# Three sparsely used experts of a mixture layer: fp32 products in column tiles, and expert matrices stored in 1 MB blocks

## The chip, the cores and the metric

The kernel runs on one core of one Trainium2 chip. The metric is device time in microseconds (us) of one execution of the whole program, the median of several runs. A profile of one execution gives the rows below.

## The reference, cut to what matters

The program is a four-layer network on 256 tokens of width 1024, all in fp32: two hybrid layers, a pooling layer with a dense feed-forward part, and an attention layer with a mixture of eight experts. The change is in the mixture alone:

```python
def moe_ffn(x, router, w_gu, w_down):        # D = 1024, N_EXPERTS = 8, TOP_K = 2, D_FF_EXPERT = 3584
    logits = (xt @ router).astype(jnp.float32)
    top_v, top_i = lax.top_k(logits, TOP_K)
    w = jax.nn.softmax(top_v, axis=-1)
    combine = jnp.einsum('tk,tke->te', w, jax.nn.one_hot(top_i, N_EXPERTS, ...))
    for e in range(N_EXPERTS):
        y = y + combine[:, e:e + 1] * swiglu(xt, w_gu[e], w_down[e])

def swiglu(x, w_gu, w_down):
    g, u = jnp.split(x @ w_gu, 2, axis=-1)
    return (jax.nn.silu(g) * u) @ w_down
```

Each expert has 42 MB of weights (w_gu 1024 x 7168, w_down 3584 x 1024), so all eight are 336 blocks of 1 MB (1,048,576 bytes). The router, evaluated on the inputs, gives the experts 63, 135, 103, 26, 69, 94, 6 and 16 tokens. The kernel takes expert 0 first (63 tokens) and sorts the rest by count: positions 0 to 7 hold 63, 135, 103, 94, 69, 26, 16 and 6 tokens.

## The kernel before

A product of fp32 matrices is made of single-pass products of split numbers. `wload` (L133) loads 1 MB of weights into a tile `raw` [128, 2048]. `wsplit` copies it in a reduced format into `whi` on ScalarE (L148) and subtracts on VectorE to get the rest, `wlo` (L149). `raw` has five buffers, `whi` and `wlo` four each. `mm3` (L182 to L184) then takes three matmuls of 512 columns: activation-hi by whi, activation-hi by wlo, activation-lo by whi. That is how tiles of 128 tokens (kind "f") work. A tile of 64 tokens (kind "h") puts the 64 hi and the 64 lo columns of its activations side by side into one stationary operand, so that two matmuls do (`prod`, L1284 and L1285); `fold` then adds the upper 64 PSUM rows to the lower (a copy on ScalarE, L1292, an add on VectorE, L1293).

An expert goes through seven chunks of 512 hidden columns. A chunk has three parts, each with two 1 MB blocks: `up1` (gate product and silu), `up2` (the other product and the multiplication, after `mid` has transposed the chunk before, L1353) and `down` (into the PSUM banks `acc`, two chunks later). This text calls one such part a step: two blocks, 24 matmuls for a tile of 128 tokens, 16 for one of 64. An expert has 21 steps. `gather` (L1253) picks an expert's tokens by a product with a selection matrix, `weigh` and `combine` (L1396 to L1409) scale its result and add it to `y`.

Experts at positions 0 to 4 have an "f" tile; the one at position 1 has an "h" tile as well (its tokens 129 to 192). Positions 5, 6 and 7 have "h" tiles. `run_experts` is a generator that stops after each step. The driving loop runs positions 0, 7, 1, 2, 3, 4 in this order, and a second generator, `light`, holds positions 5 and 6: it is advanced by two steps behind each step of position 1, and by one behind each of position 2. All blocks are loaded from SyncE's queue, in program order; a load waits there until the buffer that it writes is free. Beside the five `raw` buffers a list `K.spare` gives some loads a buffer elsewhere, during position 0 alone.

A block of w_gu is four pieces of 512 columns, so each partition gets rows of 2 KB; one of w_down is two rows of 4 KB per partition.

If a count is over a table `lim`, a branch runs more tiles. The counts above are under it in both kernels, so the branch is not taken.

Of the kernel before, what the change touches and what calls it, by code (L numbers as in the profile page):

```python
# [51 lines left out]
def _consts():  # L52
# [36 lines left out]
    for g in range(2):  # L89
        for q in range(64):  # L90
# [10 lines left out]
                ("lim", np.array([[128.0, 192, 128, 256, 256, 64, 256, 256]])),  # L101
# [58 lines left out]

class W:
# [10 lines left out]
    def __call__(self, k, c0, c1):  # L172
        hi, lo = self.parts[k // self.per]
        return hi[:, k % self.per, c0:c1], lo[:, k % self.per, c0:c1]

# [962 lines left out]
def route_order(K, pool, S):  # L1138
# [34 lines left out]
    R = wide(pool, 48, 192 + 448, name="R").rearrange("p (a b) -> p a b", a=6)  # L1173
# [16 lines left out]
class Tile:  # L1190


    def __init__(self, s0, kind):
        self.s0, self.kind = s0, kind
        self.xg, self.P, self.sb, self.sg, self.hT = None, None, False, {}, {}
# [11 lines left out]
def select(K, pool, R, p, tl, tiles=(0, 1)):  # L1207
# [5 lines left out]
    m = 64 if tl.kind == "h" else 128  # L1213
# [14 lines left out]
def gather_x(K, pool, x, R, p, tl, n, between=None):  # L1228
# [4 lines left out]
    m = 64 if half else 128  # L1233
    xg = buffer(K, pool, f"xg{n}", 0, [128, KT, m // 64, 128], F32R, dbl)
# [10 lines left out]
    for k, t in steps:  # L1245
# [12 lines left out]
        if half:  # L1258
# [6 lines left out]
def gather_w(K, pool, cw, p, tl, n):  # L1265
# [9 lines left out]
    tl.cs = K.csp.tile([128, 1], F32, name=f"cs{n}", bufs=dbl)  # L1275
# [14 lines left out]
def fold(K, a, ps):  # L1290

    K.nc.scalar.activation(a, ps[64:128, :], AF.Copy)  # L1292
    K.nc.vector.tensor_tensor(a, ps[0:64, :], a, op=OP.add)  # L1293
    return a


class Expert:
    def __init__(self, p, tiles, n0=0):
        self.p, self.tiles, self.n0 = p, [Tile(*t) for t in tiles], n0
        self.static = 0 if p == 0 else None  # L1300


def run_experts(K, pool, A, x, R, ri, cw, y, experts, hook=None, last=False):
# [5 lines left out]
    def begin(E):  # L1309
# [5 lines left out]
        E.gu = A["moe_w_gu_2"][0][ds(e, 1), :, :].rearrange("o (k p) n -> p (o k) n", p=128)  # L1315
        E.dn = A["moe_w_down_2"][0][ds(e, 1), :, :].rearrange("o (k p) n -> p (o k) n", p=128)
        for n, tl in enumerate(E.tiles):
            tl.n = E.n0 + n
# [6 lines left out]
    def up1(E, f):  # L1325
        w = W(K, E.gu[:, :, f * 512:(f + 1) * 512], KT, 512)
        for tl in E.tiles:
            ps = bank(K, "mm")
            for k in range(KT):
                prod(K, tl, ps, tl.xg[:, k], w(k, 0, 512), k == 0, k == KT - 1)  # L1330
            m = 64 if tl.kind == "h" else 128
            a = buffer(K, pool, f"sg{tl.n}", E.p * NF + f, [128, 512], F32, 2)
            nc.scalar.activation(a[:m], fold(K, a[:64], ps) if m == 64 else ps, AF.Silu)
            tl.sg[f] = a

    def up2(E, f):
        w = W(K, E.gu[:, :, FE + f * 512:FE + (f + 1) * 512], KT, 512)
        for tl in E.tiles:
            ps = bank(K, "mm")
            for k in range(KT):  # L1340
                prod(K, tl, ps, tl.xg[:, k], w(k, 0, 512), k == 0, k == KT - 1)
            m = 64 if tl.kind == "h" else 128
# [298 lines left out]
```

## Time and profile before

| | us |
|---|---|
| median of 3 runs | 2108.87 (2108.22 to 2114.42) |
| the profiled execution | 2108.73 |
| its span | 2106.8 |
| first matmul of an expert | 1098.6 |
| last addition to y, start | 2088.8 |
| PE busy | 2039.0 (97%) |
| VectorE (DVE) busy | 1605.5 (76%) |
| ScalarE (ACT) busy | 1255.6 (60%) |

The times of the trace are counted from the start of the span. The busy share of PE is not its use: matmul records overlap in the pipeline, so use has to be read from the distance between their starts.

### The profile page before, as it was taken

The page shows a single profiled execution, that of the slowest core. Times are in us where ns is not written, and L with a number is a line of the kernel's source. Part 1 is how long each engine was busy: PE and PEld are TensorE (multiplying, and loading weights), DVE is VectorE, ACT ScalarE, POOL GpSimd, SP SyncE. Part 2 cuts the span into 40 slices and gives each one's busy share as a digit, 9 for nine tenths or more (in the row PEclk, how much of TensorE's full clock was granted, in tenths as well). Part 3 has the DMA queues.
Part 4 walks back from the last instruction along what each step waited for, and adds up shares of the span by engine and source line. Part 5 has one row for each costly group of instructions (what it writes and reads, how often), then busy time and mean ns, then how long its engine had stood idle before and what let it go on. Part 6 is the DMA issues. An engine that isn't in the chain of part 4 may idle for free. (4 is left out here: it accounts for less than half of the span.)

```text
span 2106.8 us, 28987 instructions
## 1 busy us (share of the span) xinstructions
PE 2039.0 (97%) x11351; PEld 1742.8 (83%) x11351; DVE 1605.5 (76%) x1820; ACT 1255.6 (60%) x1345; POOL 35.2 (2%) x39
## 2 busy tenths in 40 slices
PE   8999999999999999999999999999999999999996
PEld 7879997888998899898788877778777878888885
DVE  7865545876555644566779899999999999898887
ACT  6644444655444444354437787887777876777773
POOL 0000000000001100000000000000000000000000
PEclk9999999999999999999989999999999999999998
DMA  8434554535555455550349979999999999999995
GB/s 312 141 100 150 174 197 165 171 121 180 187 180 192 161 186 194 162 197 21 125 160 326 357 289 374 351 371 354 365 344 326 371 366 337 345 354 351 339 366 182
DMA packets 237954, 523.75 MB, mean 249 GB/s; under 512 B 12016, under 2 KB 44144, under 8 KB 237680
## 3 DMA queue, kind: packets, MB, share of 16 engines
q1 hardware_dynamic: 237664, 521.75, 69.9%
q8 instruction: 91, 1.49, 0.3%
q14 instruction: 55, 0.45, 0.1%
q10 hardware_dynamic: 144, 0.07, 0.0%
HBM read 520.73 MB, written 1.05 MB: 248 GB/s over the span
## 5 line engine op out<-in xcount | busy, mean ns | idle before, releaser
L149 DVE TENSOR_TENSOR wlo<-raw,whi 128x2048 fp32r<-128x2048 f32 (+2 forms) x482 | 1046.1, 2193 | 265.0 <-ACT whi L148 264.6
L148 ACT ACTIVATE whi<-raw 128x2048 fp32r<-128x2048 f32 (+2 forms) x484 | 877.6, 1839 | 328.1 <-issue 70.5
L183 PE MATMUL acc<-wlo,hT 128*128 128x512 f32 x624 | 244.6, 392 | 2.7 <-DVE wlo L149 2.7
L184 PE MATMUL acc<-whi,hT 128*128 128x512 f32 x624 | 242.7, 389 | 0.0
L182 PE MATMUL mm<-xT,whi 128*128 128x256 f32 (+1 forms) x824 | 237.2, 288 | 0.8 <-ACT mqk L424 0.4
L184 PE MATMUL mm<-xT,wlo 128*128 128x256 f32 (+1 forms) x824 | 234.7, 285 | 0.0
L183 PE MATMUL mm<-xT,whi 128*128 128x256 f32 (+1 forms) x824 | 233.8, 284 | 0.3
L182 PE MATMUL acc<-whi,hT 128*128 128x512 f32 x624 | 233.2, 390 | 0.0
L183 PE MATMUL mm<-wlo,xg 128*128 128x512 f32 x448 | 176.5, 394 | 0.8 <-DVE wlo L149 0.8
L182 PE MATMUL mm<-whi,xg 128*128 128x512 f32 x448 | 175.9, 393 | 0.0
L184 PE MATMUL mm<-whi,xg 128*128 128x512 f32 x448 | 174.8, 390 | 0.2 <-DVE xg L198 0.2
L182 PEld LDWEIGHTS mm<-xT,whi 128*128 128x128 f32 (+1 forms) x824 | 155.5, 189 | 4.5 <-issue 1.1
L183 PEld LDWEIGHTS mm<-xT,whi 128*128 128x128 f32 (+1 forms) x824 | 155.6, 189 | 3.7 <-DVE xT L643 1.1
L184 PEld LDWEIGHTS mm<-xT,wlo 128*128 128x128 f32 (+1 forms) x824 | 155.6, 189 | 1.3 <-issue 0.7
L183 PEld LDWEIGHTS acc<-wlo,hT 128*128 128x128 f32 x624 | 117.2, 188 | 28.7 <-DVE wlo L149 5.6
L184 PEld LDWEIGHTS acc<-whi,hT 128*128 128x128 f32 x624 | 117.2, 188 | 24.1
L182 PEld LDWEIGHTS acc<-whi,hT 128*128 128x128 f32 x624 | 117.2, 188 | 24.0
L183 PE MATMUL mx<-xT,whi 128*128 128x256 f32 x416 | 117.7, 283 | 0.0
L184 PE MATMUL mx<-xT,wlo 128*128 128x256 f32 x416 | 117.7, 283 | 0.0
L182 PE MATMUL mx<-xT,whi 128*128 128x256 f32 x416 | 117.7, 283 | 0.0
L1285 PE MATMUL mm<-wlo,box 128*128 128x512 f32 x280 | 107.5, 392 | 0.0
L1284 PE MATMUL mm<-whi,box 128*128 128x512 f32 x280 | 107.3, 390 | 0.0
(397 smaller groups left out, 3417.2 us busy)
## 6 DMA issues: line engine op xcount, KB each, us to landing
raw<-in_moe_w_gu_dram SPq DMA_DIRECT2D x207, 1024.0 KB, 6.8
raw<-in_moe_w_down_dram SPq DMA_DIRECT2D x106, 1024.0 KB, 6.8
raw<-in_w_up_dram SPq DMA_DIRECT2D x32, 1024.0 KB, 5.8
raw<-in_w_down_dram SPq DMA_DIRECT2D x32, 1024.0 KB, 5.1
raw<-in_w_in_dram SPq DMA_DIRECT2D x26, 1024.0 KB, 5.5
raw<-in_ffn_w_gu_dram SPq DMA_DIRECT2D x22, 1024.0 KB, 5.0
spare<-in_moe_w_gu_dram SPq DMA_DIRECT2D x17, 1024.0 KB, 7.2
raw<-in_ffn_w_down_dram SPq DMA_DIRECT2D x11, 1024.0 KB, 4.7
```

Of the source, the lines that this page charges most:

```text
L148: nc.scalar.activation(h, d, AF.Copy)
L149: K.lo.tensor_tensor(l, d, h.bitcast(F32), op=OP.subtract)
L182: nc.tensor.matmul(ps, l[0], r[0], start=start, stop=False)
L183: nc.tensor.matmul(ps, l[0], r[1], start=False, stop=False)
L184: nc.tensor.matmul(ps, l[1], r[0], start=False, stop=stop)
L1284: nc.tensor.matmul(ps, x[:, 0, :], w[0], start=start, stop=False)
L1285: nc.tensor.matmul(ps, x[:, 0, :], w[1], start=False, stop=stop)
```

## The change

The experts at positions 5, 6 and 7 no longer split their weights. Position 5 has a tile of 64 tokens (kind "s"), 6 and 7 have tiles of 32 (kind "q"). Their matmuls take the raw fp32 weights and fp32 activations directly (`prod_full`, L1327), one for each 128 rows by 512 columns of weights: 8 matmuls in a step. The output of successive matmuls goes to different PSUM partitions: two places of 64 rows, or four of 32, which is a place of its own in the columns of the PE array. `fold` adds these parts up. All three now stand in `light`, and a fraction says how many light steps follow a step of each heavy expert: 0.4 for position 0 (once the first light tile is gathered), 1.35 for position 1, 0.45 for 2 to 4. What is left comes behind position 4. The spare list gives every ninth load an extra buffer over the whole layer. The host lays the expert matrices out so that each 1 MB block is contiguous, 8 KB per partition.

```diff
-                ("lim", np.array([[128.0, 192, 128, 256, 256, 64, 256, 256]])),
+                ("lim", np.array([[128.0, 192, 128, 256, 256, 64, 32, 256]])),
...
+class Raw:
+    def __init__(self, K, src, kt, n):
+        self.per = min(kt, 2048 // n)
+        self.parts = [wload(K, src[:, k:k + self.per, :], self.per, n) for k in range(0, kt, self.per)]
...
+        self.m = {"f": 128, "h": 64, "s": 64, "q": 32}[kind]
+        self.full = kind in "sq"
...
+def prod_full(K, tl, ps, c, x, w, start, stop):
+    K.nc.tensor.matmul(ps[tl.m * c:tl.m * c + tl.m], x, w, start=start, stop=stop)
...
+def fold(K, pool, a, ps, m=64):
     K.nc.scalar.activation(a, ps[64:128, :], AF.Copy)
     K.nc.vector.tensor_tensor(a, ps[0:64, :], a, op=OP.add)
-    return a
+    if m == 32:
+        b = pool.tile([32, 512], F32, name="fq")
+        K.nc.scalar.activation(b, a[32:64], AF.Copy)
+        K.nc.vector.tensor_tensor(a[0:32], a[0:32], b, op=OP.add)
+    return a[:m]
...
     def up1(E, f):
-        w = W(K, E.gu[:, :, f * 512:(f + 1) * 512], KT, 512)
+        w = (Raw if E.full else W)(K, E.gu[f], KT, 512)
         for tl in E.tiles:
             ps = bank(K, "mm")
             for k in range(KT):
-                prod(K, tl, ps, tl.xg[:, k], w(k, 0, 512), k == 0, k == KT - 1)
+                if tl.full:
+                    G = 128 // tl.m
+                    prod_full(K, tl, ps, k % G, tl.xg[:, k], w(k, 0, 512), k < G, k >= KT - G)
+                else:
+                    prod(K, tl, ps, tl.xg[:, k], w(k, 0, 512), k == 0, k == KT - 1)
...
     def down(E, f):
-        w = W(K, E.dn[:, f * 4:f * 4 + 4, :], 4, 1024)
+        w = (Raw if E.full else W)(K, E.dn[:, f * 4:f * 4 + 4, :], 4, 1024)
         for tl in E.tiles:
+            if tl.full:
+                if f == 0:
+                    tl.acc = [bank(K, "acc") for _ in range(2)]
+                for k in range(4):
+                    for h in range(2):
+                        if tl.m == 32:
+                            prod_full(K, tl, tl.acc[h], 2 * (k % 2) + (h ^ (k // 2)), tl.hT[f][:, k],
+                                      w(k, h * 512, (h + 1) * 512), f == 0, f == NF - 1)
...
-            for q in range(5):
-                for n in range(q > 0, 5):
+            for q in range(44):
+                for n in range(q > 0, 5 if q < 2 else 2):
...
-            E = [Expert(p, t) for p, t in enumerate(([F0], [F0, H(128)], [F0], [F0], [F0], [H(0)], [H(0)], [H(0)]))]
+            E = [Expert(p, t) for p, t in enumerate(([F0], [F0, H(128)], [F0], [F0], [F0], [(0, "s")], [(0, "q")], [(0, "q")]))]
...
-            light = go([E[5], E[6]])
-            for e, f in go([E[q] for q in (0, 7, 1, 2, 3, 4)], hook, True):
-                for _ in range({1: 2, 2: 1}.get(e.p, 0)):
-                    next(light, None)
+            light, done, due = go([E[5], E[6], E[7]]), 0, 0.0
+            rate = (0.4, 1.35, 0.45, 0.45, 0.45)
+            for q, (e, f) in enumerate(go([E[q] for q in (0, 1, 2, 3, 4)], hook, True)):
+                if E[5].tiles[0].xg is not None:
+                    due += rate[e.p]
+                while done < int(due) and next(light, None):
+                    done += 1
+            for _ in light:
+                pass
...
+    a["moe_gu"] = f(np.asarray(inputs["moe_w_gu_2"])[0].reshape(NE, 2, 4, 128, 14, 512)
+                    .transpose(0, 4, 1, 3, 2, 5).reshape(NE, 14, 2, 128, 2048))
+    a["moe_dn"] = f(np.asarray(inputs["moe_w_down_2"])[0].reshape(NE, 14, 2, 128, 1024)
+                    .transpose(0, 1, 3, 2, 4).reshape(NE, 14, 128, 2048))
```

The instructions of the layers ahead of the mixture keep their order on every engine. Inside it, three places show what moves. The first is PE in the expert of position 1, before: `xgr` are the activations of its "f" tile, `box` those of an "h" tile in `light`, `xg` its own "h" tile.

```order
L1284 MATMUL mm<-whi,xg_11451 128x512
L1285 MATMUL mm<-wlo,xg_11451 128x512
L182 MATMUL mm<-whi,xgr_11032 128x512
L1284 MATMUL mm<-whi,box_10899 128x512
L1353 MATMUL mm<-ident,box_10900 128x64 x4
L183 MATMUL mm<-wlo,xgr_11032 128x512
L184 MATMUL mm<-whi,xgr_11032 128x512
```

The same expert after the change (L1318 and L1319 are now the "h" tile's two matmuls, L210 to L212 the "f" tile's three, L1407 the transposes, L1284 the gathering, L1327 the fp32 products on raw weights):

```order
L1318 MATMUL mm<-whi,box_10276 128x512
L1319 MATMUL mm<-wlo,box_10276 128x512
L1407 MATMUL mm<-ident,box_10277 128x64 x4
L1327 MATMUL mm<-raw,box_10278 64x512 x4
L1327 MATMUL mm<-spare_11037,box_10278 64x512 x4
L1327 MATMUL mm<-raw,box_10278 64x512 x8
L1284 MATMUL mm<-P,x 128x32 x16
L1304 MATMUL mm<-identr,Pr 128x128 x2
L1306 MATMUL mm<-cw,Pr 128x2 x2
L1407 MATMUL mm<-ident,sg_10753 128x128 x4
```

So a light step is 8 matmuls in place of 16 (here two steps stand behind each other); they stand in runs between the heavy tile's matmuls, 106 such runs in all.

The second place is PE at the end of the layer. Before, the last rows ahead of the branch are those of position 4 and its combination:

```order
L182 MATMUL acc<-whi,hT_17109 128x512
L183 MATMUL acc<-wlo,hT_17109 128x512
L184 MATMUL acc<-whi,hT_17109 128x512
L1407 MATMUL mm<-ye,PT_15994 128x512 x2
L1408 MATMUL mm<-ye,PT_15994 128x512 x2
```

After, the light steps that are left stand behind them (L1481 and L1482 are the combination):

```order
L1482 MATMUL mm<-ye,PT_14664 128x512 x2
L1327 MATMUL mm<-raw,box_10278 32x512 x8
L1407 MATMUL mm<-ident,box_10277 128x32 x4
L1327 MATMUL mm<-raw,box_10278 32x512 x8
L1327 MATMUL acc<-raw,hTl 32x512 x4
L1407 MATMUL mm<-ident,box_10277 128x32 x4
L1327 MATMUL acc<-raw,hTl 32x512 x4
L1327 MATMUL acc<-spare_16221,hTl 32x512 x4
L1327 MATMUL acc<-raw,hTl 32x512 x12
L1481 MATMUL mm<-ye,PTl_11093 128x512 x4
L1482 MATMUL mm<-ye,PTl_11093 128x512 x4
```

The third place is SyncE's queue in the middle of the layer, with what each load waits for (register instructions between the loads are left out). Before, the buffer of a load was always last read by VectorE:

```order
L133 DMA raw<-in_moe_w_gu_dram 128x4x512 [waits DMAHW1_49,DVE_49]
L133 DMA raw<-in_moe_w_gu_dram 128x4x512 [waits DMAHW2_49,DVE_49]
L133 DMA raw<-in_moe_w_down_dram 128x2x1024 [waits DMAHW3_49,DVE_49]
L133 DMA raw<-in_moe_w_down_dram 128x2x1024 [waits DMAHW4_49,DVE_49]
L133 DMA raw<-in_moe_w_gu_dram 128x4x512 [waits DMAHW5_49,DVE_49]
```

After, a load into a buffer that held a light block waits for PE:

```order
L133 DMA raw<-in_moe_gu_dram 128x2048 [waits DMAHW7_49,DVE_49]
L133 DMA raw<-in_moe_dn_dram 128x2048 [waits DMAHW0_49,PE_49]
L133 DMA raw<-in_moe_dn_dram 128x2048 [waits DMAHW1_49,PE_49]
L133 DMA raw<-in_moe_gu_dram 128x2048 [waits DMAHW2_49,DVE_49]
L133 DMA raw<-in_moe_gu_dram 128x2048 [waits DMAHW3_49,DVE_49]
L133 DMA raw<-in_moe_dn_dram 128x2048 [waits DMAHW5_49,DVE_49]
L133 DMA raw<-in_moe_dn_dram 128x2048 [waits DMAHW6_49,PE_49]
```

## Rows read from the trace of the kernel before

**Rows 1.** The page: the span in 40 slices (granted PE clock in tenths, GB/s).

```profile
PEclk9999999999999999999989999999999999999998
DMA  8434554535555455550349979999999999999995
GB/s 312 141 100 150 174 197 165 171 121 180 187 180 192 161 186 194 162 197 21 125 160 326 357 289 374 351 371 354 365 344 326 371 366 337 345 354 351 339 366 182
```

**Rows 2.** Busy us (and instructions) of each engine in stretches of the mixture.

```profile
core 0: us, PE busy (x) PEld busy (x) DVE busy (x) ACT busy (x) POOL busy (x), PEclk, DMA share, GB/s
1250.00:2050.00 800.00, 786.73 (x3630) 640.22 (x3629) 734.35 (x519) 600.12 (x460) 0.00 (x0) 1.00 0.98 354
...
1326.00:1650.00 324.00, 319.97 (x1446) 256.34 (x1445) 303.66 (x224) 249.92 (x204) 0.00 (x0) 1.00 0.98 354
...
1760.00:2060.00 300.00, 300.00 (x1391) 248.33 (x1391) 260.25 (x158) 213.47 (x146) 0.00 (x0) 1.00 0.97 352
```

**Rows 3.** Who waited for whom, 1760 to 2060 us (total, times, longest).

```profile
DVE wlo L149 <- ACT whi L148: 29.9, 39, 3.0
ACT whi L148 <- PE mm L184: 22.5, 28, 2.6
...
ACT whi L148 <- DMA raw<-in_moe_w_gu_dram: 2.3, 3, 1.4
```

**Rows 4.** Groups by line, 1760 to 2060 us: busy, mean ns, idle before.

```profile
L149 DVE TENSOR_TENSOR wlo<-raw,whi 128x2048 fp32r<-128x2048 f32 x101 | 228.4, 2287 | 30.1 <-ACT whi L148 29.9
L148 ACT ACTIVATE whi<-raw 128x2048 fp32r<-128x2048 f32 x101 | 191.5, 1915 | 39.6 <-PE mm L184 22.5 <-PE acc L184 14.5 <-DMA raw<-in_moe_w_gu_dram 2.3
```

**Rows 5.** What SyncE's queue waited for, 1250 to 2050 us.

```profile
SPq L133 <- DVE wlo L149: 593.9, 253, 6.0
```

**Rows 6.** Tiles: the "f" tile of position 1, and position 5's and 6's last products.

```profile
L182 PE MATMUL mm<-whi,xgr x112: 387/389/501, 1326.6 to 1648.5; 128*128 128x512 f32 x112
L1284 PE MATMUL acc<-whi,box x112: 387/389/485, 1393.2 to 1713.1; 128*128 128x512 f32 x112
```

**Rows 7.** DMA, 1250 to 2050 us: packets and issues (KB, us to landing).

```profile
DMA packets 119364, 283.39 MB, mean 354 GB/s; under 512 B 4304, under 2 KB 4304, under 8 KB 119314
...
raw<-in_moe_w_gu_dram SPq DMA_DIRECT2D x180, 1024.0 KB, 6.9
raw<-in_moe_w_down_dram SPq DMA_DIRECT2D x90, 1024.0 KB, 6.7
```

**Rows 8.** DMA, 497 to 499 us, when `poolc`, 8 KB per partition, is loaded.

```profile
DMA packets 114, 0.84 MB, mean 422 GB/s; under 512 B 8, under 2 KB 8, under 8 KB 14
...
q1 hardware_dynamic: 114, 0.84, 101.0%
```

**Rows 9.** Timeline of PE, single-pass matmuls of 512 columns (start, us).

```profile
1101.00 0.39 PE L184 MATMUL mm<-whi,xg 128*128 128x512 f32 x1
...
1101.91 0.39 PE L182 MATMUL mm<-whi,xg 128*128 128x512 f32 x1
```

**Rows 10.** Timeline of PE: fp32 products of 256 columns (x2 records each).

```profile
682.39 0.59 PE L719 MATMUL mx<-poolc,x 128*128 128x256 f32 x2
682.82 0.59 PE L719 MATMUL mm<-poolc,x 128*128 128x256 f32 x2
```

**Rows 11.** Timeline of PE around transposes that use 64 rows of the array.

```profile
1375.17 0.39 PE L1285 MATMUL mm<-wlo,box 128*128 128x512 f32 x1
1375.49 0.46 PE L1353 MATMUL mm<-ident,box 64*128 64x64 f32 x4
1375.87 0.50 PE L1285 MATMUL mm<-wlo,box 128*128 128x512 f32 x1
1376.21 0.39 PE L1284 MATMUL mm<-whi,box 128*128 128x512 f32 x1
```

**Rows 12.** Groups by line, 1300 to 1900 us: the folding of a 64-token tile.

```profile
L1293 DVE TENSOR_TENSOR fu<-mm,fu 64x512 f32<-64x512 f32 x23 | 15.5, 675 | 0.0
L1292 ACT ACTIVATE fu<-mm 64x512 f32<-64x512 f32 x23 | 13.6, 593 | 6.4 <-PE mm L1285 4.9 <-DVE box L1344 0.9
```

More of the change, by code (lines that the diff above doesn't have):

```diff
@@ L174, in __call__, with __init__, __getitem__ @@
         return hi[:, k % self.per, c0:c1], lo[:, k % self.per, c0:c1]
+class Packed:
+    def __init__(self, ap, per, k0=0, k1=None, n=slice(None)):
+        self.ap, self.per, self.k0, self.n = ap, per, k0, n
+    def __getitem__(self, at):
+        _, k, n = at
+        n = self.n if n == slice(None) else n
+        b, o = divmod(self.k0 + k.start, self.per)
+        q = k.stop - k.start
+        if o + q > self.per:
+            return Packed(self.ap, self.per, self.k0 + k.start, None, n)
+        return self.ap[b][:, o:o + q, n]
 def rows_kt(src):
@@ L1212, in select @@
         tl.Pr = pool.tile([128, 2, 128], F32R, name="Pr", bufs=2)
-    m = 64 if tl.kind == "h" else 128
+    m = tl.m
     src = K.iota[:, None, :m].to_broadcast([128, 128 // m, m])
@@ L1232, in gather_x @@
     nc = K.nc
-    m = 64 if half else 128
-    xg = buffer(K, pool, f"xg{n}", 0, [128, KT, m // 64, 128], F32R, dbl)
+    m = tl.m
+    xg = buffer(K, pool, f"xg{n}", 0, *([[128, KT, m], F32] if tl.full else [[128, KT, m // 64, 128], F32R]), dbl)
     if between is None:
@@ L1348, in mid @@
             sg = tl.sg[f]
-            m = 64 if tl.kind == "h" else 128
-            h = buffer(K, pool, f"hT{tl.n}", E.p * NF + f, [128, 4, m // 64, 128], F32R, 2)
+            m = tl.m
+            h = buffer(K, pool, f"hT{tl.g}", E.p * NF + f,
+                       *([[128, 4, m], F32] if tl.full else [[128, 4, m // 64, 128], F32R]), 2)
             pt = bank(K, "mm")[:, :4 * m].rearrange("p (a b) -> p a b", a=4)
@@ L1392, in weigh @@
     def weigh(tl, halves=(0, 1)):
+        if K.weighed is not None and K.weighed[0] is not tl:
+            K.weighed[1]()
+        K.weighed = tl, lambda: combine(tl, halves)
         a, b = K.ye
@@ L1401, in combine @@
     def combine(tl, halves=(0, 1)):
+        if K.weighed is None or K.weighed[0] is not tl:
+            return
+        K.weighed = None
         a, b = tl.y
@@ new lines, in hook @@
+                if 4 <= i < len(ahead) + 4:
+                    p, n = ahead[i - 4]
+                    gather(K, ep, x, R, cw, p, E[p].tiles[n], f"l{p}" if p > 1 else n)
+            light, done, due = go([E[5], E[6], E[7]]), 0, 0.0
[5 more added lines that the diff above has]
+                    done += 1
@@ L1549, in build @@
         nc.scalar.dma_start(K.ident, A["ident"])
-        half = K.cons.tile([128, 2], F32, name="mhalf")
+        half = K.cons.tile([128, 4], F32, name="mhalf")
         K.mhalf = half[:, 0:1]
@@ L1570, in build @@
                 n2g = K.cons.tile([128, 16], F32, name="n2g")
-                gb = K.cons.tile([16, 2], F32, name="gb")
+                gb = half[:16, 2:4]
                 def consts():
```

88 lines of the change are left out of this document (50 added, 38 removed).

## The prediction

> **What bounds the kernel now.** The slices come first. From the 21st on, the rate of the DMA doubles and stays near 350 GB/s to the end, at full PE clock [rows 1]: that is the mixture, about 990 us from its first matmul (1098.6) to its last addition (2088.8). The change touches nothing else, so the question is what sets the pace in this stage.
>
> The table of stretches shows two engines at their limit together: over 800 us the DMA engines are busy 0.98 of the time at 354 GB/s, and PE 787 of 800 us [rows 2]. The share of the DMA is the time its packets take, so 354/0.98 = 361 GB/s is what it can do with these rows of 2 and 4 KB, or 2.90 us for a block of 1,048,576 bytes; 336 blocks need 974 us. PE's busy time overlaps itself, so I take the distance of starts: four matmuls of 512 columns in 0.91 us, 0.2275 each [rows 9]. A heavy step has 24, 5.46 us for two blocks.
>
> In the stretch where only 128-token tiles run (1760 to 2060), 300 us x 352 GB/s are 100.7 blocks, 2.98 us each, 5.96 for a step: PE's 5.46 and 0.5 of transposes, gathering and combining. The waits there say who is last: VectorE waits for ScalarE (29.9 us), ScalarE for PE to give a `whi` back (22.5), and hardly for a load (2.3) [rows 3]. So PE is the narrower by a little, the DMA next to it, and the splits (1915 and 2287 ns per block [rows 4]) are not the limit. SyncE's queue waits 593.9 us for buffers [rows 5]: the loads run as soon as a buffer is free.
>
> **What the change costs and saves, step by step.**
>
> *Splitting.* 126 of the 336 blocks lose their copy and subtraction: 126 x 1.9 = 241 us of ScalarE, 126 x 2.29 = 288 us of VectorE. The folding of a 32-token tile adds a copy and an add, 28 times at most 0.59 and 0.68 us [rows 12], 19 us. Neither engine sets the pace, so this counts as nothing; if the splits were the limit, the 288 us would be the upper end of a gain, but VectorE's own idle time is spent waiting for PE.
>
> *Loads.* Every block becomes 128 rows of 8 KB. The one such load in the trace is `poolc`: in its 2 us, 100 of 114 packets are of 8 KB or more, at 422 GB/s and a share of 1.01 [rows 8], 418 GB/s, 2.51 us per block against 2.90. Two microseconds are a short sample and PE leaves it alone; with the 0.97 share of the busy stretch it is 2.59, which I take, since it is the same kind of row. The ends are 2.51 (no loss) and 2.98 (no gain).
>
> *PE.* A light step was 16 matmuls, 16 x 0.2275 = 3.64 us. It becomes 8 fp32 products. The trace has fp32 products of 256 columns: each makes two records, and the next product starts 0.43 us later [rows 10], so 0.86 for 512 columns, against 0.455 for the two matmuls that one replaces. No matmul of the trace stands beside another in other columns of the array, so the cost has two ends: 0.86 us if each has the array alone, and 0.43 (64 tokens, two places) or 0.215 (32 tokens, four) if they overlap fully. That is 8 x 0.86 = 6.9 us a step, or 3.44 and 1.72. I take full overlap, since the four places hold different output rows and no product waits for another's result; the serial end stays in the range.
>
> The Trainium skill, "TensorEngine Tiling (Array Packing)", Key Properties, says that column tiles work independently and in parallel, and that changing the tiling mode drains the engine; its Theoretical Speedup allows 2 and 4. "TensorE: Matmul & The Clock Gate", Part 3, measured 2.38 for three column tiles; at that efficiency the sum below would come out near 2085, an estimate. No run here shows two column tiles at once; on the drain the trace agrees [rows 11].
>
> *Changes of mode.* Between 128-row matmuls and transposes on 64 rows the spacing is not 0.23: 0.32 before, then 0.38 for four small ones, and 0.34 behind the next matmul [rows 11]. Four such transposes cost some 0.3 us more than their own work. The light products stand in 106 runs over 63 steps, 106 x 0.3 / 63 = 0.5 us a step. With the transposes, gathering and combining of the light experts (0.4) a light step is 3.44 + 0.9 = 4.3 us for position 5 and 2.6 for 6 and 7.
>
> *The order.* I sum by stretches, each at the slower of PE and DMA.
> - Position 0: 21 steps x 5.96 = 125, and 1.6 light ones, 7: 132 us (DMA 45 blocks, hidden).
> - Position 1: 21 steps of 40 matmuls, 9.1 + 0.5 = 9.6, are 202; 28.4 light steps, 19.4 of position 5 (83) and 9 of position 6 (23): 308 us of PE. Its 99 blocks x 2.59 = 256 hide.
> - Positions 2 to 4: 62 steps x 5.96 = 370 and 27.9 light ones x 2.6 = 73, 443 on PE; 180 blocks x 2.59 = 466 of DMA. 466.
> - The rest: 6 light steps, 12 blocks, 31, and 5 for the last products and the combination: 36.
>
> Together 942. The same sum for before gives 125 (position 0), 42 x 2.90 = 122 (position 7), 202 + 42 x 4.1 = 374 (position 1 and `light`, in the trace 1326.6 to 1713.1 with the first part of position 2 in it [rows 6]), 63 x 5.96 = 375: 996, the trace has 990. I take the difference to 990: 48 us. Against the profiled execution (2108.73; span 2106.8, 1.9 beside it; 0.1 under the median of the runs) this is 2061, rounded up to **2062 us**.
>
> *What the queue does.* A load into a light block's buffer now waits for PE, and all loads behind it wait too, the heavy ones among them, for whose splits ScalarE waits. A load lands after 6.7 to 6.9 us [rows 7]; a heavy block is out of its buffer 1.9 + 2.3 us later, about 11. A light one must wait for PE to end the heavy step ahead of it, 6 us and the products, 14. Mixed, five or six buffers turn over every 12 us, 2.2 us a block, under 2.59. So it costs nothing as long as PE isn't far behind; where PE sets the pace the queue waits anyway.
>
> **Rivals.**
> - *Two at a time.* A product is two records [rows 10], and the records start one after another [rows 9 to 11]. If the second must wait for the first of the same product, and the next product can only start behind it, then just the second record of one and the first of the next overlap: 0.43 us whatever the number of places. Light steps are 4.3 us for all three: 132 + 324 + (370 + 120 = 490, PE now over the DMA) + 36 = 982, 2100; without the loss in the queue no better. The Trainium skill, "TensorE: Matmul & The Clock Gate", Part 3, states this order of starts and ends; the trace agrees, as far as it has no tiles to show otherwise. Range 2093 to 2125.
> - *Little overlap (the other side).* With a share of it, 0.61 us a product, a step is 5.8: 134 + 367 + 532 + 40 = 1073, 2192. Alone in the array, 7.8 a step: 138 + 424 + 588 + 52 = 1202, 2321. The point of decision: 125 + 202 + 370 + 36 = 733 and 57.9 light steps must make 990, 4.4 us a step, (4.4 - 0.9) / 8 = 0.44 us a product. For it speaks that a fp32 product alone costs 0.86; against it, that PE would have to refuse work for other columns.
> - *No faster loads.* If 361 GB/s is what memory gives and not what the rows of 2 KB cost, a block stays at 2.98: 132 + 308 + 536 + 41 = 1017, 2136. The Trainium skill, "DMA: Bandwidth & Descriptors", Where 436 GB/s comes from, has a limit of about 358 GB/s of memory for a core; the trace differs, with 422 [rows 8], if for 2 us. That speaks against it.
>
> **How the numbers follow.** Full overlap with faster loads: 0.56, from 2040 (2.51 us a block and a little less loss on PE: 452 + 35 in place of 466 + 36, and 5 to 10 us) to 2098 (2.78 a block, half way to no gain: 500 + 38), with 0.04 below 2040. Two at a time 0.19, little overlap 0.19 (a third of it up to 2190), no faster loads 0.06. The predicted time is that of the first. The range, 2040 to 2190, leaves out 0.04 below and 0.13 above. A measurement can tell about 0.3%, 6 us, from no change. Faster by more (under 2102.5): 0.55 of the first and 0.07 of the second, 0.62. Within: 0.01 and 0.09 of these, 0.10. Slower: 0.03 and the last two, 0.28.
>
> **What would show it.** In the profile after, starts of L1327 records should overlap: a light step in 1.8 us for 32 tokens, 3.5 for 64; two at a time shows 3.5 in both, the serial case 6.9. In positions 2 to 4 the DMA share should be about 0.97 at near 405 GB/s and PE should wait for `raw`; in position 1 PE should have no idle time and the rate of the DMA should fall to some 340 GB/s. VectorE's busy time in the mixture falls by a quarter or more. Wrong is the prediction if PE's records of L1327 stand one after another, if the rate of the DMA stays under 370 while its share is near 1, or if SyncE's queue waits for PE while the DMA is idle in positions 2 to 4.

## The result, and the profile after

The change makes the kernel slower: 2127.93 us, median of 5 runs (2122.95 to 2132.57), against 2108.22 (2106.32 to 2114.42), a ratio of 1.0086 (95% interval 1.0061 to 1.0111). The profiled execution took 2122.95 us, its span is 2121.1. The forecast was 2062 and faster.

The page first (granted PE clock and busy share of the DMA in tenths, GB/s, 40 slices), for [rows 1]:

```profile
PEclk9999999999999999999989999999999999999997
DMA  8424555425554555451347778787899999999886
GB/s 310 140 100 159 193 180 183 160 95 199 180 197 160 188 189 179 157 179 37 128 180 305 269 304 330 289 326 301 350 383 358 365 354 373 384 383 376 345 335 252
```

Then the stage after, cut at the first matmul of each position and behind the last gate or up product of position 4, for [rows 2]. The stretches are position 0, position 1, positions 2 to 4, and the rest up to the last addition to y:

```profile
core 0: us, PE busy (x) PEld busy (x) DVE busy (x) ACT busy (x) POOL busy (x), PEclk, DMA share, GB/s
1095.90:1215.30 119.40, 119.04 (x594) 100.30 (x593) 99.44 (x101) 80.87 (x61) 0.00 (x0) 1.00 0.72 276
1215.30:1527.80 312.50, 309.49 (x1453) 200.66 (x1451) 157.80 (x160) 124.89 (x129) 0.00 (x0) 0.98 0.80 317
1527.80:2051.80 524.00, 475.25 (x2225) 324.51 (x2222) 362.69 (x268) 294.41 (x235) 0.00 (x0) 0.97 0.93 367
2051.80:2105.70 53.90, 41.78 (x216) 20.21 (x214) 25.88 (x34) 15.12 (x20) 0.00 (x0) 0.91 0.80 309
```

The forecast had 132, 308, 466 and 36 us. So 58 us too much are in positions 2 to 4 and 18 in the rest. In positions 2 to 4 neither PE (475 of 524) nor the DMA (0.93) is at its limit.

Who waited for whom in positions 2 to 4 (total, times, longest), for [rows 3], and below it what SyncE's queue waited for, for [rows 5]:

```profile
DVE sg L1397 <- PE mm L212: 50.5, 13, 6.9
...
ACT hT L225 <- PE mm L1407: 45.9, 14, 5.7
ACT sg L1382 <- PE mm L212: 41.4, 16, 8.5
ACT fu L1332 <- PE mm L1327: 32.7, 9, 7.7
PEld mm L211 <- DVE wlo L149: 31.3, 29, 2.1
ACT box L1332 <- PE mm L1327: 30.1, 9, 8.9
ACT whi L148 <- DMA raw<-in_moe_gu_dram: 28.5, 8, 6.0
PE mm L211 <- DVE wlo L149: 21.4, 22, 1.8
```

```profile
SPq L133 <- DVE wlo L149: 269.9, 102, 7.0
SPq L133 <- PE mm L1327: 103.3, 35, 7.1
SPq L133 <- PE acc L1327: 31.6, 16, 3.8
```

Before, in the 300 us of [rows 3], ScalarE waited 37 us (22.5 and 14.5) for PE to give a split block back, which means that it was ahead, and 36 us (18.1 and 17.9) for results of PE. These rows of the same view show it:

```profile
ACT sg L1333 <- PE mm L184: 18.1, 16, 3.1
ACT hT L197 <- PE mm L1353: 17.9, 9, 3.8
ACT whi L148 <- PE acc L184: 14.5, 17, 1.7
DVE sg L1344 <- PE mm L184: 6.6, 9, 1.4
```

After, in 524 us, ScalarE waits for *results* of PE, 45.9 + 41.4 + 32.7 + 30.1 = 150 us, and hardly for a block to come back. VectorE waits 50.5 us for one kind of result (6.6 before), PE waits for split weights, and the queue waits 135 us for light products.

The column tiles, in PE's timeline after (start, us, records). A light part for 64 tokens, then one for 32:

```profile
1248.05 3.65 PE L1327 MATMUL mm<-raw,box 128*64 128x512 f32 x16
...
1902.48 0.61 PE L210 MATMUL acc<-whi,hT 128*128 128x512 f32 x2
1903.03 1.07 PE L1327 MATMUL acc<-raw,hTl 128*32 128x512 f32 x8
1904.02 0.50 PE L211 MATMUL acc<-wlo,hT 128*128 128x512 f32 x1
```

Sixteen records (eight products) last 3.65 us, so a product advances PE by 0.43; eight records for 32 tokens (four products) last 1.07, and the next heavy matmul starts 0.99 behind the first of them. One product alone would be 0.86, twice the 0.43 of 256 columns [rows 10]. The overlap is complete.

### The profile page after: what moved, and what is told of

Read it like the earlier page. It is cut to its first block, busy times and chain, and to the rows that moved or that the text cites. A ratio compares the mean times of both kernels' runs of the same rounds, so it can differ in the third digit from the quotient of the medians.

```text
span 2121.1 us, 28472 instructions
## 1 busy us (share of the span) xinstructions
PE 2008.5 (95%) x11351; PEld 1594.7 (75%) x11351; DVE 1348.1 (64%) x1716; ACT 1033.7 (49%) x1226; POOL 34.8 (2%) x39
## 5 line engine op out<-in xcount | busy, mean ns | idle before, releaser
L149 DVE TENSOR_TENSOR wlo<-raw,whi 128x2048 fp32r<-128x2048 f32 (+2 forms) x345 | 745.9, 2177 | 329.3 <-ACT whi L148 325.9
L148 ACT ACTIVATE whi<-raw 128x2048 fp32r<-128x2048 f32 (+2 forms) x347 | 624.9, 1823 | 363.5 <-DMA raw<-in_moe_gu_dram 80.8
L211 PE MATMUL mm<-wlo,xg 128*128 128x512 f32 x560 | 232.2, 415 | 21.5 <-DVE wlo L149 21.4
L212 PE MATMUL acc<-whi,hT 128*128 128x512 f32 x624 | 244.5, 392 | 0.0
L210 PE MATMUL acc<-whi,hT 128*128 128x512 f32 x624 | 237.1, 395 | 5.7 <-ACT whi L148 5.7
L210 PE MATMUL mm<-whi,xg 128*128 128x512 f32 x560 | 229.6, 410 | 11.7 <-ACT whi L148 8.0
L210 PE MATMUL mm<-xT,whi 128*128 128x256 f32 (+1 forms) x824 | 237.2, 288 | 0.8 <-ACT mqk L452 0.4
L212 PE MATMUL mm<-xT,wlo 128*128 128x256 f32 (+1 forms) x824 | 234.7, 285 | 0.0
L212 PE MATMUL mm<-whi,xg 128*128 128x512 f32 x560 | 224.7, 401 | 0.4 <-DVE xg L226 0.4
L210 PEld LDWEIGHTS mm<-xT,whi 128*128 128x128 f32 (+1 forms) x824 | 155.6, 189 | 4.5 <-issue 1.1
L211 PEld LDWEIGHTS mm<-wlo,xg 128*128 128x128 f32 x560 | 109.0, 195 | 65.6 <-DVE wlo L149 31.3
L212 PEld LDWEIGHTS mm<-xT,wlo 128*128 128x128 f32 (+1 forms) x824 | 155.6, 189 | 1.3 <-issue 0.7
L210 PEld LDWEIGHTS mm<-whi,xg 128*128 128x128 f32 x560 | 108.7, 194 | 53.9 <-ACT whi L148 14.5
L210 PEld LDWEIGHTS acc<-whi,hT 128*128 128x128 f32 x624 | 116.9, 189 | 41.4 <-issue 10.8
L212 PEld LDWEIGHTS acc<-whi,hT 128*128 128x128 f32 x624 | 118.1, 189 | 23.9
L212 PEld LDWEIGHTS mm<-whi,xg 128*128 128x128 f32 x560 | 109.2, 195 | 22.6 <-DVE xg L226 0.8
L211 PE MATMUL mx<-xT,whi 128*128 128x256 f32 x416 | 117.7, 283 | 0.0
L212 PE MATMUL mx<-xT,wlo 128*128 128x256 f32 x416 | 117.7, 283 | 0.0
```

Of the source, the lines that this page charges most:

```text
L148: nc.scalar.activation(h, d, AF.Copy)
L149: K.lo.tensor_tensor(l, d, h.bitcast(F32), op=OP.subtract)
L210: nc.tensor.matmul(ps, l[0], r[0], start=start, stop=False)
L211: nc.tensor.matmul(ps, l[0], r[1], start=False, stop=False)
L212: nc.tensor.matmul(ps, l[1], r[0], start=False, stop=stop)
```

## Experiments

Times are medians; in brackets stand the ratio to the kernel before on the same chip and its 95% interval. The lengths of positions are read as above, each from one profiled execution.

**1. The storage.** The blocks alone, on the kernel before:

```diff
-        E.gu = A["moe_w_gu_2"][0][ds(e, 1), :, :].rearrange("o (k p) n -> p (o k) n", p=128)
-        E.dn = A["moe_w_down_2"][0][ds(e, 1), :, :].rearrange("o (k p) n -> p (o k) n", p=128)
+        E.gu = [Packed(A["moe_gu"][ds(e, 1)].rearrange("o c q p (k n) -> (o c) q p k n", k=4)[c], 4) for c in range(2 * NF)]
+        E.dn = Packed(A["moe_dn"][ds(e, 1)].rearrange("o b p (k n) -> (o b) p k n", k=2), 2)
...
-        w = W(K, E.gu[:, :, f * 512:(f + 1) * 512], KT, 512)
+        w = W(K, E.gu[f], KT, 512)
```

> The kernel before with the new storage alone: every expert block is 1 MB in one piece, rows of 8 KB; order, splitting and matmuls stay. If the larger rows are what makes the loads faster (2.65 us a block in the profile after, 2.90 before), the part of the mixture that waited for loads gets shorter: position 7, 42 blocks, from 122 to about 111 us, and little where PE is the narrower (5.96 us a step of two blocks): 2085 to 2100 us. If the rate after came from something else, for instance from fewer splits beside it, no change, 2106 to 2112 us.

And the kernel after with the old storage (these lines back):

> The kernel after with the old storage, rows of 2 and 4 KB; the order of all matmuls is the same as after. If the service of the DMA engines bounds positions 2 to 4 after the change, their 183 blocks at 2.90 in place of 2.65 us add 46 us: about 2170 us. If it is the queue, which waits for buffers that PE holds, a slower block adds to every load's way only in part: 2135 to 2160 us. If the storage does nothing, 2123 to 2133 us.

2109.77 us (1.0008, 0.9994 to 1.0021) and 2127.72 (1.0104, 1.0074 to 1.0134): the storage does nothing to the time of either kernel. The stretches, first 1760 to 2060 us of the kernel before with blocks:

```profile
1760.00:2060.00 300.00, 300.00 (x1391) 248.35 (x1390) 259.79 (x159) 213.61 (x147) 0.00 (x0) 1.00 0.93 351
```

and positions 2 to 4 of the kernel after with the old rows:

```profile
1532.90:2054.00 521.10, 472.78 (x2225) 322.90 (x2222) 362.47 (x268) 294.42 (x235) 0.00 (x0) 0.97 1.00 369
```

About the same bytes per us as without the edit (352 and 367 GB/s), at a share of 0.93 where [rows 2] have 0.97 for this stretch, and of 1.00 where the kernel after has 0.93. A share near 1 did not mean that the DMA set the pace.

**2. What PE and the held buffers cost.** Light products on a resident tile (`K.held`, a part of the layer's input), then without their loads:

```diff
-    K.nc.tensor.matmul(ps[tl.m * c:tl.m * c + tl.m], x, w, start=start, stop=stop)
+    K.nc.tensor.matmul(ps[tl.m * c:tl.m * c + tl.m], x, K.held, start=start, stop=stop)
...
-        self.parts = [wload(K, src[:, k:k + self.per, :], self.per, n) for k in range(0, kt, self.per)]
+        self.parts = [K.held.rearrange("p (a b) -> p a b", a=1)] * (kt // self.per)      # no_light_load
```

> The light products read a tile that is resident (the layer's input) in place of their loaded block; the loads stay, but nothing reads the block, so its buffer is free when it has landed. Left out: the results of positions 5 to 7 are not the reference's. Bytes, matmuls and splits stay. If the queue loses its time in waiting for PE to give light buffers back (128 us of such waits between 1527.8 and 2051.8, DMA share 0.93, PE waiting 60 us), positions 2 to 4 fall from 524 to 475 to 490 us and the whole to 2070 to 2090 us. If the DMA engines' service or the cost of changing between light and heavy matmuls is the limit, or if it is the order with its rest at the end, no change: 2117 to 2130 us.

> As the run before this one, but the light blocks are not loaded at all: 210 blocks in place of 336. Left out: the results of positions 5 to 7. What is left is PE's own time. By the terms of the prediction 132 + 308 + 443 + about 20 for the end, so positions 2 to 4 take 445 to 455 us and the whole is near 2020 us. If light steps cost PE more than those terms (changes of mode, short runs), positions 2 to 4 stay over 490 us and the whole over 2060 us.

2086.69 us (0.9896, 0.9878 to 0.9915), and 2034.81 in its one run. Without light loads positions 2 to 4 take 445 us, with PE busy in all of them:

```profile
1525.80:1971.20 445.40, 445.40 (x2189) 321.94 (x2186) 356.88 (x264) 296.32 (x233) 0.00 (x0) 1.00 0.76 287
```

The forecast had 443 for PE, so no PE term failed. With the resident tile alone, positions 2 to 4 take 498 us, 26 of the 79 over PE's 445 regained but more than the 475 to 490 expected, and the rest 41 in place of 54.

The resident tile changes more than the buffers. Its products need not wait for a block to land, and PE's order comes out another way: in positions 2 to 4 the light products stand in 45 runs in place of 58. I matched each load of the kernel after with its use to see which of this can matter. In positions 2 to 4 no light product began sooner than 2.7 us after its block had landed, so there PE did not wait for light loads. In the rest the last 7 of 14 light blocks were read within 1.0 us of landing, for instance here:

```profile
2085.00 1.06 PE L1327 MATMUL acc<-raw,hTl 128*32 128x512 f32 x8 [0.54 <-DMA raw<-in_moe_dn_dram]
```

So the gain in the rest can be that of loads which nothing waits for any more.

**3. Other rings, other fractions.** Buffers divided, four for heavy blocks and two for light ones, with light loads on GpSimd's queue or on SyncE's; without the extra buffer; other fractions:

```diff
-    raw = K.spare.pop(K.loads)() if K.loads in K.spare else K.raw.tile([128, 2048], F32, name="raw", tag="raw")
+    raw = ring(K, light)                                    # own_queue, own_buffers
-            last = K.nc.sync.dma_start(v[:, o, :], src[:, o, :])
+            last = (K.nc.gpsimd if light else K.nc.sync).dma_start(v[:, o, :], src[:, o, :])   # own_queue
...
-            for q in range(44):
+            for q in range(5):                              # no_spare
-            rate = (0.4, 1.35, 0.45, 0.45, 0.45)
+            rate = (0.4, 2.2, 0.25, 0.25, 0.25)             # balance
+            rate = (0.4, 3.0, 0.0, 0.0, 0.0)                # all_in_1
```

> From the first light load on, heavy loads have four buffers to themselves and light ones two (the fifth of the ring and the extra one); the light loads are issued from GpSimd's queue, so no heavy load waits behind a light one or for a buffer that a light product reads. All results are computed. If the loss is in the one queue and the shared ring, this takes it away as the resident tile did: SyncE has no wait for PE L1327 any more, positions 2 to 4 fall from 524 to 480 to 505 us and the whole to 2080 to 2100 us. If it was the resident tile's earlier PE order that helped there, or if the heavy loads need all buffers, no change or slower: 2120 us and more.

> The same division of buffers (four for heavy loads, two for light ones), but all loads stay in SyncE's queue. If what costs is that heavy loads need a buffer that PE holds, this gives most of the gain, 2085 to 2105 us. If it is the order of the queue, a light load still waits for PE to end the light step ahead of it and holds up the heavy ones behind it: 2110 to 2135 us, well over the version with two queues.

> The kernel after, but every ninth load has an extra buffer during position 0 alone; from position 1 on there are five. If the time that a buffer is held sets the rate of the loads in positions 2 to 4, one in nine fewer buffers makes them slower, by up to a tenth of 524 us: 2140 to 2170 us, with a lower DMA share there (under 0.90). If buffers don't set it, no change, 2120 to 2133 us.

> The kernel after with other fractions of light steps: 2.2 behind a step of position 1 (1.35 after), 0.25 behind one of positions 2 to 4 (0.45). By PE's own time and 2.65 us a block the two stretches are then 355 and 409 us in place of 312 and 524, the end 54: 2040 us. If a block takes 2.86 us wherever light ones are among them, because they hold the queue, position 1 has 134 blocks, 383 us, and positions 2 to 4 155 blocks, 443 us: 826 in place of 836, about 2115 us. If the light steps left at the end are what costs, the end gets shorter by 10 us or so and nothing else changes.

> The kernel after with all light steps in position 1: three behind each step there, none in positions 2 to 4 (0.4 in position 0 stays). Position 1 then has PE work of 202 + 19.4 x 4.3 + 42 x 2.6 = 394 us and 165 blocks, 412 us at the 2.5 us of loads that stand close together, 437 at 2.65: 415 to 450 us. Positions 2 to 4 have heavy steps alone, 62 x 5.96 = 370, and the end is that of before, 21 us. If a light step costs little beside heavy steps of 9.6 us and much beside those of 5.96, the stage is 119 + 430 + 370 + 21 = 940: 2045 to 2080 us. If a light step costs its 4 to 5.5 us wherever it stands, as a block that is held for PE would have it, about 2100 us.

In this order: own queue 2166.97 us (1.0268, 1.0250 to 1.0286), own buffers 2201.67 (1.0448, 1.0419 to 1.0478), no extra buffer 2121.94 (1.0067, 1.0050 to 1.0084), 2.2 and 0.25 light steps 2125.53 (1.0073, 1.0055 to 1.0091), all in position 1 2110.70 (1.0012, 0.9996 to 1.0028). The first two lost most in position 1 (367 and 374 us in place of 312), which has the most light blocks for their two buffers; in positions 2 to 4 the own queue took 501 us, the own buffers 521. To go without the extra buffer cost nothing, which speaks against a plain shortage of buffers. With 0.25 positions 2 to 4 took 477 us where PE needs 409 and 155 blocks at 2.65 need 411: 66 us over both, which no theory so far explains. With all light steps in position 1, that position took 447 us, and the whole was over both forecasts.

**4. ScalarE's waits, and less work for PE.** The fold on a resident tile, the same with the products on one, and two of three heavy products:

```diff
-            a = buffer(K, pool, f"sg{tl.g}", E.p * NF + f, [128, 512], F32, 2)
+            a, ps = buffer(K, pool, f"sg{tl.g}", E.p * NF + f, [128, 512], F32, 2), K.held if tl.full else ps
...
-            m = tl.m
+            m, ps = tl.m, K.held if tl.full else ps         # free_fold, free_both
...
+    elif K.cut:                                             # less_pe, from position 2 on
+        nc.tensor.matmul(ps, x[:, 0, :], w[0], start=start, stop=False)
+        nc.tensor.matmul(ps, x[:, 0, :], w[1], start=False, stop=stop)
```

> The kernel after, but the folding and the silu of the light tiles (and the product behind them) read a resident tile in place of the PSUM bank, so that ScalarE and VectorE do the same work and never wait for a light product. Left out: the results of positions 5 to 7. Loads and light buffers stay as after. If it is ScalarE's order that costs (it waits for L1327 with the splits of the next heavy blocks behind it: 40 of 400 us between 1560 and 1960), positions 2 to 4 fall from 524 to 480 to 500 us and the whole to 2080 to 2105 us. If the held buffers are the cause by themselves, no change: 2117 to 2133 us.

> Both at once: the light products read a resident tile (as in the run with no buffer held for PE) and their folding reads one too. Left out: the results of positions 5 to 7. If the two waits cost apart from each other, positions 2 to 4 come near the larger of PE's 445 and the loads' 450 to 466 us, the whole to 2040 to 2065 us. If one is only the shadow of the other, as with no buffer held: 2080 to 2092 us.

> The kernel after, but the heavy tiles leave out the third of the three products (activation-lo by whi) from position 2 on. PE's own time in positions 2 to 4 falls from 445 to about 327 us; the loads, their buffers, the splits and the light steps stay. If the loss comes from two nearly equal resources with few buffers between them, the loads alone are left: 180 blocks at 2.5 to 2.65 us, 450 to 477, the whole 2050 to 2080 us. If it is the time for which a block is held that sets the rate whatever PE does (16 us over 5.6 buffers, 2.86 a block), positions 2 to 4 stay at 505 to 524 us.

2117.81 (1.0043, 1.0023 to 1.0063), 2086.78 (0.9887, 0.9856 to 0.9919) and 2106.53 us (one run). Waiting for the folding is a shadow: it is worth 10 us alone, nothing beside the resident tile. With a third of the heavy matmuls gone positions 2 to 4 still take 508 us, and PE is idle in a fifth of them (at a granted clock of 0.88):

```profile
1528.20:2036.00 507.80, 402.95 (x1749) 260.15 (x1746) 362.46 (x267) 290.93 (x234) 0.00 (x0) 0.88 0.94 378
```

So neither PE's work, nor the size of a row, nor one buffer in nine sets the pace of positions 2 to 4. What these kernels share is the order in which ScalarE's instructions stand in the program. Here is a place in position 3 of the kernel after; `whi` is a split, the other rows need a result of PE, and `sg0_14492` needs the product of the two blocks right above it (14457, 14463):

```
925 L148 ACTIVATE whi_14457<-raw_14455 128x2048
926 L148 ACTIVATE whi_14463<-spare1_14461 128x2048
927 L225 ACTIVATE hT0_14513<-mm_14514 128x4x128
928 L1382 ACTIVATE sg0_14492<-mm_14467 128x512
929 L148 ACTIVATE whi_14523<-raw_14521 128x2048
```

In the trace these two results are waited for, one behind the other:

```profile
1812.97 0.60 ACT L225 ACTIVATE hT<-mm 128x512 fp32r<-128x512 f32 x1 [4.88 <-PE mm L1407]
1815.51 0.60 ACT L1382 ACTIVATE sg<-mm 128x512 f32<-128x512 f32 x1 [1.94 <-PE mm L212]
```

ScalarE stands at 928 until PE has used up every split block, and only then splits the next one. I count this for each such row: blocks split so far, less the blocks that PE has begun by the end of that result. Over positions 2 to 4 the mean is 1.0 after; before it was 3.0, 2.7 and 1.6 in positions 2, 3 and 4.

**5. Splits ahead.** The next heavy step is loaded and split before the work of this one, and that work's instructions are held behind the splits:

```diff
+    def fetch(k, E, f):
+        at = seq.index((k, E, f))
+        w = made.pop(at) if at in made else make(k, E, f)
+        if not E.full and E.p >= 1 and at + 2 < len(seq):
+            made[at + 1] = make(*seq[at + 1])
+            K.ahead = K.split                               # its last copy and subtraction
+        return w
+
     def up1(E, f):
-        w = (Raw if E.full else W)(K, E.gu[f], KT, 512)
+        w = fetch(0, E, f)
+        with behind(K, K.ahead):
+            up1_(E, f, w)
```

> The kernel after, but from position 1 on the blocks of a heavy step are loaded and split ahead of the work of the step before: the instructions of ScalarE and VectorE that need a result of PE stand behind the next step's splits in their queues. Nothing else changes. In the order of the kernel after, ScalarE comes to an instruction that needs a result of PE when it has split on average only 1.0 heavy block more than PE needs for that result (none more in 18 of 74 places of positions 2 to 4); here it is 1.8 (4 of 76). If that order is what couples PE and the loads, positions 2 to 4 fall from 524 to 470 to 500 us and the whole to 2070 to 2100 us. If the loads themselves set the rate there (2.84 us a block, whatever was tried), no change: 2117 to 2133 us.

> The same with the old storage (rows of 2 and 4 KB). With the order of the kernel after, the storage made no difference (2127.7 against 2127.9). If the order had hidden it, it shows now: a load that is issued over 5 us ahead takes 2.51 us with the large rows and 2.71 with the small ones, 183 blocks in positions 2 to 4: 20 to 35 us slower than the run before this one. If the loads give the same mean rate with both rows anyway, no difference again.

> The run with splits ahead, and light steps at 2.2 behind a step of position 1 and 0.25 behind one of positions 2 to 4. By PE's own time, 5.96 a heavy and 2.6 a light step, positions 2 to 4 need 409 us, by the loads 155 blocks at 2.5 to 2.65, 388 to 411; without splits ahead they took 477. If the order is the cause, 415 to 445 us there, 355 to 384 in position 1, the whole 2050 to 2090 us and faster than the kernel before. If not, 2115 to 2130 us as with these fractions alone.

2090.07 us (0.9917, 0.9890 to 0.9945), 2092.37 (0.9917, 0.9890 to 0.9944) and 2075.10 (0.9829, 0.9798 to 0.9859). The new order is worth 38 us, and all three beat the kernel before; the small rows still cost nothing that shows. In the run with 0.25 positions 2 to 4 took 458 us, over the 445 expected. Positions 2 to 4 and the rest with splits ahead, and ScalarE's waits there:

```profile
1524.30:2017.00 492.70, 463.56 (x2225) 321.10 (x2222) 358.76 (x265) 293.90 (x234) 0.00 (x0) 0.98 0.96 385
2017.00:2069.40 52.40, 43.84 (x216) 21.31 (x214) 27.07 (x35) 16.35 (x21) 0.00 (x0) 0.84 0.82 326
```

```profile
ACT whi L148 <- DMA raw<-in_moe_gu_dram: 53.7, 23, 8.7
ACT fu L1332 <- PE mm L1327: 28.5, 8, 8.9
ACT sg L1415 <- PE mm L212: 21.4, 13, 3.5
...
ACT box L1332 <- PE mm L1327: 14.4, 7, 4.1
...
ACT hT L225 <- PE mm L1439: 8.8, 6, 3.4
...
DVE sg L1429 <- PE mm L212: 2.9, 2, 2.3
```

The four waits for results fell from 150 to 73 us, and what ScalarE waits for most is now a load: the right neighbour. But ScalarE's is not the only order that changed. VectorE's instructions stand behind the next splits as well, and its wait of 50.5 us for a result is down to 2.9; the heavy loads are issued a step earlier against the light ones; and PE's light runs, 59 of them in place of 58, stand in other places. So the run shows what the order of the program costs, and not which engine's order.

**6. Controls.** The kernel before with splits ahead from position 2 on; splits ahead with the resident tile; splits ahead with all light steps in position 1 (the edits of 5, with those of 2 and 3):

> The kernel before with the same splits ahead, from position 2 on. There ScalarE comes to a result of PE with 2.5 blocks split on average beyond what PE needs for it (now 3.0), and it waits mostly for PE to give a split block back [rows 3], so PE sets the pace. If the order was the fault of the kernel after alone, no change: 2103 to 2113 us. If splits ahead help any kernel of this shape, 2070 to 2095 us, and the fp32 products have no part in the gain of the runs with splits ahead.

> Splits ahead, and the light products read a resident tile, so that no buffer is held for PE. Left out: the results of positions 5 to 7. With the order of the kernel after this gave 41 us, but its order had changed too (2.3 blocks ahead in position 2). If held buffers still cost with splits ahead, another 15 to 30 us: 2060 to 2075 us, positions 2 to 4 at 465 to 480. If the gain there was that of the order, as with splits ahead alone: 2083 to 2097 us.

> Splits ahead, all light steps in position 1 (3.0 behind each step there). Position 1 has 165 blocks at 2.5 to 2.75 us, 412 to 454 us (447 without splits ahead), positions 2 to 4 heavy steps alone, 370 us (402 without, with the light steps left over in them), the end 21: 2045 to 2085 us, near the run with 2.2 and 0.25 (2075). If many light steps in a row cost more than single ones, over 2095 us.

2112.12 us (1.0011, 0.9997 to 1.0025), 2049.06 (0.9719, 0.9686 to 0.9752) and 2080.33 (0.9851, 0.9827 to 0.9875). The kernel before gains nothing. It was ahead already (3.0, 2.7 and 1.6 blocks, see 4), and the edit adds about half a block, so this shows that to be further ahead is worth nothing there; how the kernel before would do at 1.0 was not tried. The second is faster than both of its forecasts. By position:

```profile
1097.60:1216.80 119.20, 118.99 (x593) 100.28 (x592) 99.27 (x100) 82.61 (x62) 0.00 (x0) 1.00 0.75 288
1216.80:1527.30 310.50, 309.40 (x1485) 199.28 (x1483) 164.49 (x164) 128.37 (x131) 0.00 (x0) 1.00 0.82 332
1527.30:1990.40 463.10, 450.02 (x2226) 323.73 (x2223) 359.47 (x265) 295.19 (x233) 0.00 (x0) 0.99 0.98 404
1990.40:2028.80 38.40, 34.00 (x184) 19.97 (x182) 23.05 (x32) 13.55 (x19) 0.00 (x0) 0.96 1.01 411
```

But for position 0 (119 for 132) this is the forecast's table: 310 for 308, 463 for 466 at 404 GB/s and a share of 0.98, 38 for 36. That the loads are the limit now, as it said, is argued and not shown: PE is busy for 450 of the 463 us, and this kernel was not run with the small rows.

Does the held buffer cost by itself? The two steps add up (38 and 41 us alone, 79 together), but the resident tile changed the order too: ScalarE's, and PE's, whose light products stand in 34 runs with both edits and in 59 with splits ahead. By position it can be seen: length in us, and in brackets the blocks ahead.

| | position 2 | position 3 | position 4 | rest |
|---|---|---|---|---|
| after | 184.7 (1.2) | 169.3 (1.0) | 170.0 (1.0) | 53.9 |
| no buffer held | 169.0 (2.3) | 168.2 (0.9) | 160.7 (1.2) | 40.8 |
| splits ahead | 175.7 (1.8) | 163.2 (2.0) | 153.8 (1.7) | 52.4 |
| both | 159.9 (2.8) | 155.2 (2.4) | 148.0 (2.5) | 38.4 |

In position 3, where ScalarE's lead stayed, the resident tile gave 1 us. It gives 13 to 14 in the rest in both pairs, where products no longer wait for their loads. Single positions vary by some 5 us (with splits ahead and the old rows position 3 took 168.2 in the same order), so the 8 us that it gives in position 3 beside splits ahead say little. How much of the 41 us is the held buffer, and how much the order, the loads or fewer changes of mode, stays open: a kernel with released buffers and an unchanged order was not tried.

## Why the prediction was wrong, point by point

The time, 2127.93 us, lies inside the stated range by luck alone: the range reached to 2190 for rivals that did not happen.

- *Column tiles.* Right: full overlap, 0.43 and 0.215 us a product. "Two at a time" and "little overlap" fall. The Trainium skill, "TensorEngine Tiling (Array Packing)", Theoretical Speedup, allows 2 and 4, and the trace agrees.
- *Changes of mode.* Right: start to start, a light record comes 0.32 us behind a heavy matmul in place of 0.23, a heavy one 0.52 behind a light one in place of 0.43, and the next heavy one 0.34 behind that in place of 0.23. In all a run of light products costs 0.34 us over the plain spacing (the median of 50 runs), 0.3 by the forecast. The sum for PE came out too (445 for 443).
- *Position 1.* Right, 312.5 for 308. Position 0 took 119 in place of 132: the forecast gave it 125 before the light steps, though in the trace before it lasted 109, from the first product (1098.6) to the first of position 7 (1207.6).
- *Positions 2 to 4, 466 us, "each at the slower of PE and DMA".* **This step failed**, by 58 us. The stretch has two resources of nearly equal need (445 and 463 by the runs), and the sum took for granted that each runs freely beside the other. Without the light loads PE alone took its 445, so what failed is the overlap: 31 of the 58 us went with the order of the program (524 to 493 with splits ahead), and 30 more with the resident tile on top (493 to 463), which changes several things at once.
- The paragraph *What the queue does* saw one coupling, the buffers held for PE, and put it at nothing. Its numbers were too small: matched load by load over positions 2 to 4 (issue, landing, start of the copy, end of the subtraction), a heavy block stayed in its buffer for 16.0 us (7.8 to land, 3.1 until ScalarE came, 5.1 for the split), not 11; a light one 16.1, not 14. At 5.6 buffers that is 2.9 us a block, not 2.2. But this time is no cause by itself. Without the extra buffer the same matching gives 14.2 and 13.9 us, with five buffers again 2.8 a block: the time that a block is held followed the pace.
- The other one it did not have: in *Splitting*, the splits count "as nothing" because the engines have time. They have time, but in their queues results of PE stand ahead of the next split. The view behind [rows 3] had the sign of it, 36 us of waits for results in the rows shown above, beside the 22.5 that the forecast read. The order cost 38 us, as splits ahead show. Both edits together gave 79 us; the whole missed by only 66, since position 0 came out 13 shorter.
- *The rest*, 36 us, was 54. It is 37 to 45 in the four runs whose light products read a resident tile, and 52 with splits ahead alone. So 9 to 17 of those 18 us go with the light blocks: by their landing, which PE waits for there, or by the buffers that they hold. The runs do not tell these apart.
- *Loads.* 2.59 us a block is right only where nothing else holds them (463 us for 180 blocks, 2.57). But the 2.90 that stood against it was no limit: with splits ahead the old rows move as much in the same stretch,

```profile
1522.40:2020.10 497.70, 463.56 (x2226) 320.06 (x2222) 358.66 (x265) 294.90 (x234) 0.00 (x0) 0.98 1.02 381
```

  381 GB/s or 2.75 us a block. The first part of the prediction read a share of 0.98 [rows 2] as a DMA at its limit. "No faster loads" fits the time (2136) by accident: its mechanism, a memory limit at 361 GB/s, fell with 404 GB/s over 463 us. The Trainium skill, "DMA: Bandwidth & Descriptors", Where 436 GB/s comes from, has a limit of about 358; this run differs, with 404.
- What the prediction named as proof against itself, SyncE's queue waiting for PE while the DMA is not full in positions 2 to 4, is what the trace shows.

## What to carry to other kernels

Where two resources come out nearly equal, "the slower of the two" is a lower bound: look for what couples them, in-order queues first, and see how far each instruction that waits for a result stands behind the work that must run ahead. A DMA share near 1 is no proof of a limit: try another row size first and see if the rate moves with it. Here fp32 column tiles pay (1.7% under the kernel before with splits ahead and more light steps in position 1), but not by themselves.

## What the runs showed that was not expected

- fp32 products of two records each overlap fully in column tiles: eight records for four tiles in 1.07 us, sixteen for two tiles in 3.65.
- The DMA's busy share did not tell how near a limit was: 352 GB/s stood at 0.97 with small rows, 351 at 0.93 with rows of 8 KB, and 404 GB/s at 0.98 with rows of 8 KB.
- Nine kernels with the same light steps in position 3, and 0.5 to 1.1 blocks ahead in ScalarE's order there, took 167.5 to 172.4 us for it, whatever was changed of rows, buffers, queues, folds or PE's work. Splits ahead moved it to 163.2 with rows of 8 KB and to 168.2 with the old ones, so it is the three positions together, and not this one, that show the order's worth.
